# Delta rule of a block kernel: where the inverse of 32 x 32 diagonal blocks is formed, and one level of block products taken out

## The chip, the cores and the metric

The program runs on one core of a Trainium2 chip. The metric is the device time of one execution in microseconds (us); for the kernel before it is the median of three runs.

## The reference, cut to what matters

The program is one pass of a three-layer block network over 512 tokens of width 1024. Its first layer mixes a windowed attention with a gated delta rule of eight heads; later stages are a mixture of experts, two more mixers and feed-forward layers. The change is in the delta rule alone. In the reference it works in chunks of 64 tokens: from keys, a gate and a decay it forms a strictly lower triangular matrix A per chunk and head, and needs the inverse of the unit triangular matrix I + A:

```python
a_mat = jnp.where(tril_strict, jnp.einsum('nbhid,nbhjd->nbhij', kbeta, kc) * decay_mat, 0.0)
eye = jnp.eye(CHUNK, dtype=jnp.float32)
t_mat = lax.linalg.triangular_solve(eye + a_mat, jnp.broadcast_to(eye, a_mat.shape),
                                    left_side=True, lower=True, unit_diagonal=True)
u = jnp.einsum('nbhij,nbhjd->nbhid', t_mat, vc * bc[..., None])
w = jnp.einsum('nbhij,nbhjd->nbhid', t_mat, kbeta * jnp.exp(gcum)[..., None])
```

`u` and `w` then enter a recurrence over the chunks that carries a 128 x 128 state.

## The kernel before, in words

The kernel takes chunks of 128 tokens, so four chunks make the 512 tokens, and every per-chunk matrix of a head lies in one tile of 128 partitions x 512 columns, chunk c in columns 128c to 128c + 127. `dn_head(h)` computes one head. It is a generator: each `yield` hands back a weight, and `first_mixer` weaves the eight heads with the attention's generator by these weights. The first part of a head, up to `yield None`, projects q, k and v (three weight slabs of 128 x 1024, each 24 matmuls on 512 columns, L295), normalizes them, and forms `at`, the transposed triangular matrix of all four chunks (L551). The second part inverts, runs the recurrence and writes `ob[h]`. The second part of head h - 1 is woven into the first part of head h, and behind the three projections of head h in the program's text.

The inverse is built from small blocks to large ones. GpSimd inverts the 16 x 16 diagonal blocks: SP stores `at` to DRAM (`blk[0]`, L560) and loads the 32 diagonal blocks back with four DMAs, one block per partition (`sub`, L565). Fifteen steps of a multiply and a subtract on 32 partitions (L571, L573; at most 64 elements each) leave the inverses. Four DMAs store them to the diagonal blocks of a second DRAM tensor that is zero elsewhere (L575), and one DMA loads all of it as tile `t` (L577). TensorE transposes `t` into `tt` (L496, `tokmajor`), and two levels follow, i = 4 (blocks of 16 to 32) and i = 5 (32 to 64). A level is: GpSimd masks `at` to the off-diagonal blocks of that size (`xm`, L555), four chunk products of `xm` and `t` on TensorE (`pcps`, L547), a copy on ScalarE (`ty`), four products of `ty` and `tt`, a subtraction from `tt` on VectorE, a transposition of `tt` on TensorE and a copy to `t` on ScalarE. A float32 product of 128 columns shows as two instructions, so a set of four products shows as eight. A last level, 64 to 128, works on the one block that is left (L603, L609).

The products of the weights use a split of every float32 into two parts: a slab is loaded by SP into one of two `wraw` buffers (L278), cast by ScalarE (`whi`, L282), the rest formed by VectorE (`wlo`, L286); `whi` and `wlo` have two buffers each. SP's queue is worked off in order: a DMA that waits holds all behind it.

The order of each engine's instructions is fixed when the program is built. A planner goes through all instructions with the order in the text as their rank, and gives an engine the first in rank of those that it takes to be ready by then. So an instruction that stands late in the text can be put early, when what it needs is there and its engine is free; the order doesn't change while the program runs.

Of the kernel before, what the change touches and what calls it, by code (L numbers as in the profile page):

```python
# [22 lines left out]
F32 = mybir.dt.float32  # L23
# [4 lines left out]
OP = mybir.AluOpType  # L28
# [3 lines left out]
P = 128  # L32
S = 512
# [44 lines left out]
def _consts():  # L78
    p = np.arange(P)
    f = np.float32  # L80
    eye = (p[:, None] == p[None, :]).astype(f)
    neg = lambda ok: np.where(ok, f(0), f(NEG)).astype(f)
    c = {}
    c["ident"] = eye
    c["m_up"] = neg(p[:, None] <= p[None, :])
    c["m_lo"] = neg(p[:, None] >= p[None, :])
    c["m_prev"] = neg(p[None, :] >= p[:, None])
    c["m_res"] = neg((p[:, None] // 32 == p[None, :] // 32) & (p[:, None] >= p[None, :]))
    c["tri"] = (p[:, None] <= p[None, :]).astype(f)
    c["half"] = (p[:, None] // 64 == np.arange(2)[None, :]).astype(f)  # L90
    for i in range(7):
        b = 1 << i
        ok = (p[:, None] // (2 * b) == p[None, :] // (2 * b)) & (p[:, None] // b % 2 == 0) & (p[None, :] // b % 2 == 1)
        c[f"lv{i}"] = ok.astype(f)
    x = np.arange(3 + 512)
    c["un1"] = (x[None, :] - 3 == 4 * p[:, None]).astype(f)
    x = np.arange(12 + 512)
    c["un2"] = (x[None, :] - 12 == 16 * (p[:, None] % 32) + p[:, None] // 32).astype(f)
    return c


_CONSTS = _consts()
_COFF = {}
_n = 0
# [114 lines left out]
class Kern:  # L219
# [230 lines left out]
        self.hb = t("hb")  # L450
        nc.vector.tensor_scalar(self.hb, self.beta, 0.5, None, op0=OP.mult)

    @staticmethod
    def diag(t, c):

        a = t[:, c * P : (c + 1) * P]
        return bass.AP(a.tensor, a.offset, [[16 * S + 16, 8], [S, 16], [1, 16]])

    def dn_head(self, h):

        nc, dl, pa = self.nc, self.dl, self.pa

        def T(tag, dt=F32):
            return dl.tile([P, S], dt, tag=tag, name=tag, bufs=2 if tag in DN2 else 1)
# [11 lines left out]
        for j in range(3):  # L476
# [4 lines left out]
            w = lambda i: self.V("conv_w", i * 24 + j * 8 + h)  # L481
# [5 lines left out]
            o = T("s" + "qkv"[j])  # L487
# [22 lines left out]
        r = dl.tile([P, 8], F32, tag="rqk", name="rqk", bufs=2)  # L510
# [39 lines left out]
        at, aq = T("at"), T("aq")  # L550
# [5 lines left out]
            return x  # L556


        blk, eng = self.blk[h % 2], self.sub_engine
        nc.sync.dma_start(blk[0], at)  # L560
        x = self.sm.tile([P, S], F32, tag="sq", name="sub", bufs=2)
        lm = dl.tile([32, 64], F32, tag="lm", name="lm")
        La, Lt = (x[0:32, i * 256 : (i + 1) * 256].rearrange("p (i k) -> p i k", k=16) for i in range(2))
        for c in range(4):
            nc.sync.dma_start(La[8 * c : 8 * c + 8], self.diag(blk[0], c))  # L565
        eng.memset(Lt, 0.0)
        eng.memset(x[0:32, 256:512:17], 1.0)
        for j in range(15):
            n, w = 15 - j, j + 1
            m = lm[0:32, 0 : n * w].rearrange("p (i k) -> p i k", k=w)  # L570
            eng.tensor_tensor(m, La[:, j, j + 1 :][:, :, None].to_broadcast([32, n, w]),  # L571
                              Lt[:, j, 0:w][:, None, :].to_broadcast([32, n, w]), op=OP.mult)
            eng.tensor_sub(Lt[:, j + 1 :, 0:w], Lt[:, j + 1 :, 0:w], m)  # L573
        for c in range(4):
            nc.sync.dma_start(self.diag(blk[1], c), Lt[8 * c : 8 * c + 8])  # L575
        tt, t_ = T("tt"), T("t")
        nc.sync.dma_start(t_, blk[1])  # L577
        nc.vector.tensor_mul(aq, per_chunk(sk, sq_), dec)
        yield 0.9
        rowmul(qd, sq_, [self.egc[:, c, h : h + 1] for c in range(4)])  # L580
# [2 lines left out]
        nc.vector.tensor_tensor(c4(bv), c4(pv), colb(self.hb), op=OP.mult)  # L583
        yield 0.5
        yield None
        with self.tc.issue_after(self.last_mm.ins):
            ps = tokmajor(t_)
        nc.scalar.copy(tt, ps)
        yield 0.2
        for i in (4, 5):  # L590
            x = masked(i)
            y = T("ty")
            nc.scalar.copy(y, per_chunk(x, t_))
            yield 0.9
            nc.vector.tensor_sub(tt, tt, per_chunk(y, tt))
            yield 0.9
            nc.scalar.copy(t_, tokmajor(tt))
            yield 0.2

        a, b = slice(0, 64), slice(64, 128)  # L600
# [16 lines left out]
        for c in range(4):  # L617
            t = slice(c * P, (c + 1) * P)
# [19 lines left out]
        for c in range(4):  # L638
            t = slice(c * P, (c + 1) * P)
# [14 lines left out]
        r = self.rsqrt(dl, v, 4, "or")  # L654
# [9 lines left out]
        z, th = T("cy"), T("cth")  # L664
# [238 lines left out]
    def first_mixer(self):  # L903
        nc, tc = self.nc, self.tc
        with ExitStack() as c0:
# [4 lines left out]
            with ExitStack() as c1:  # L910
                self.pa = c1.enter_context(self.pool("pmix", 3, PSUM))
                self.ptag = "da"

                hi, lo = self.wslab(None, D, raw=self.raw0)
                ps = self.pm.tile([P, S], F32, tag="mm", name="mm")
                for k in range(KD):
                    self.split(self.x[k], self.xh[k], self.xl[k], self.V("norm_mix", k))
                    w = slice(k * P, (k + 1) * P)
                    self.gemm(ps, hi[:, w], lo[:, w], self.xh[k : k + 1], self.xl[k : k + 1], 1, first=k == 0, last=k == KD - 1)
                for k in range(KD):  # L920
                    self.square_step(k)
                self.lead = []
                self.lead = [ps, self.xgemm("w_dn", 1)]
                self.norm_end()
                self.dk = dk = c1.enter_context(self.pool("dk", 1))
                self.dl = c1.enter_context(self.pool("dl", 1))
                self.at = at = c1.enter_context(self.pool("at", 1))
                self.mb = {}

                def load(n):  # L930
                    o, w = _COFF[n]
                    t = dk.tile([P, w], F32, tag="craw", name="craw", bufs=1)
                    nc.scalar.dma_start(t, self.I["consts"][:, o : o + w])
                    return t

                for n in ("m_up", "m_res", "m_lo", "m_prev", "lv4", "lv5"):
                    self.mb[n] = dk.tile([P, P], BF, name="b" + n)
                    nc.gpsimd.tensor_copy(self.mb[n], load(n))
                for n in ("tri",):
                    w = _COFF[n][1]  # L940
                    self.mb[n] = dk.tile([P, w], F32, name="b" + n)
                    nc.scalar.dma_start(self.mb[n], self.I["consts"][:, _COFF[n][0] : _COFF[n][0] + w])
                self.on = [at.tile([P, S], F32, name=f"on{g}") for g in range(3)]
                self.stat = [at.tile([P, 4, 2, 2], F32, name=f"stat{g}") for g in range(3)]
                dram = c1.enter_context(self.pool("blk", 1, bass.MemoryType.DRAM))
                self.blk = [[dram.tile([P, S], F32, name=f"blk{i}{j}") for j in range(2)] for i in range(2)]
                z = self.sm.tile([P, S], F32, tag="sq", name="zsq")
                nc.gpsimd.memset(z, 0.0)
                for i in range(2):
                    nc.scalar.dma_start(self.blk[i][1], z)  # L950
                self.sub_engine = nc.gpsimd
                self.cin = self.dl.tile([P, S + 4], F32, name="cin")
                nc.gpsimd.memset(self.cin[:, 0:4], 0.0)
                self.gqk = at.tile([P, 1], F32, name="gqk")
                nc.vector.tensor_mul(self.gqk, self.V("q_norm"), self.V("k_norm"))
                self.mask0 = at.tile([P, 4 * P], BF, name="mask0")
                for i, n in enumerate(("m_prev", "m_lo", "m_prev", "m_lo")):
                    nc.gpsimd.tensor_copy(self.mask0[:, i * P : (i + 1) * P], self.mb[n])
                def heads():

                    gen = [self.dn_head(h) for h in range(8)]

                    def first(h):
                        c = next(gen[h])
                        while c is not None:
                            yield c
                            c = next(gen[h])

                    for h in range(8):
                        for _ in range(3):  # L970
                            yield next(gen[h])
                        if h == 0:
                            self.dn_scalars()
                            yield from first(h)
                        else:
                            yield from self.interleave((first(h), 1.0), (gen[h - 1], 1.0))
                    yield from gen[7]

                self.weave((heads(), DN_T), (self.attention(), AT_T))
# [1166 lines left out]
```

## Time and profile before

| what | value |
|---|---|
| median of three runs | 2274.68 us (2271.39 to 2280.24) |
| the profiled execution, its time | 2271.66 us |
| its span, first to last instruction | 2269.9 us |
| TensorE busy | 2164.8 us, 95% of the span |
| VectorE, ScalarE, GpSimd busy | 1488.8, 966.8, 438.9 us |
| mean granted clock of TensorE | 0.982 |
| substitution of the eight heads on GpSimd | first instruction at 82.2 us, last at 645.6 us |

The 1.8 us between the span and the profiled execution's time lie around the instructions. PE is TensorE's matmuls, DVE VectorE, ACT ScalarE, POOL GpSimd, and SPq the DMA queue of SyncE. Matmuls are pipelined: one on 512 columns is shown as 0.39 us long, while the next starts 0.23 us after it. So a set's price is read from start to start rather than from the durations.

### The profile page before, as it was taken

The numbers are of one execution on the slowest core, as the hardware profiler recorded it, in microseconds if no ns is written. First come the engines' busy times: TensorE is split into PE (matmuls) and PEld (weight loads), VectorE is DVE, ScalarE is ACT, GpSimd is POOL, SyncE is SP. The second block draws the span as 40 slices with busy tenths as digits, with TensorE's granted clock in tenths as the row PEclk, the third lists the DMA queues.
The fourth block names the chain that finished last, engine by engine and source line by source line (L and its number), as shares of the span: only waits on it lengthen the run. The fifth ranks groups of instructions, "written<-read, shape, count | busy, mean of one in ns | idle before, by whom it ended". The sixth has DMA issues, their size and how long they took to land.

```text
span 2269.9 us, 28779 instructions
## 1 busy us (share of the span) xinstructions
PE 2164.8 (95%) x10718; PEld 1722.2 (76%) x10718; DVE 1488.8 (66%) x2674; ACT 966.8 (43%) x1594; POOL 438.9 (19%) x616
## 2 busy tenths in 40 slices
PE   8999999999999998999897899999999889999997
PEld 6777777878777886565686677788888778888886
DVE  6766666666755446775689877847477567777533
ACT  4434434444343234565455454424334235444321
POOL 1222012022021013101327049700230220000000
PEclk9999999999999999899998999999999999999998
DMA  4221121211212246799321012233223113232332
GB/s 156 67 61 54 66 67 49 74 58 48 75 43 79 93 143 244 271 360 313 117 91 59 29 41 90 93 96 99 85 96 94 55 34 107 94 101 93 98 94 87
DMA packets 83299, 231.14 MB, mean 102 GB/s; under 512 B 18576, under 2 KB 22288, under 8 KB 83152
## 3 DMA queue, kind: packets, MB, share of 16 engines
q1 hardware_dynamic: 78048, 217.02, 28.8%
q0 software_dynamic: 2944, 10.49, 1.5%
q10 hardware_dynamic: 2160, 1.71, 0.3%
q8 instruction: 87, 1.43, 0.3%
q14 instruction: 60, 0.49, 0.1%
HBM read 215.89 MB, written 12.65 MB: 101 GB/s over the span
## 4 chain that ended last, share of the span: by engine, by line
PE 38%; DVE 10%; ACT 2%; issue 1%; POOL 0%; DVEq 0%; ACTq 0%; POOLq 0%
PE mm L295 34%; DVE wlo L286 2%; DVE cvps L1702 2%; DVE fy L1778 1%; PE po L1653 1%; DVE xl L306 1%; PE psc L1622 0%; PE st L1480 0%; ACT whi L282 0%; PE gps L1926 0%; PE ppt L1646 0%; DVE fe L1773 0%; DVE t L2035 0%; PE mm L1996 0%; PE mm L1997 0%
## 5 line engine op out<-in xcount | busy, mean ns | idle before, releaser
L295 PE MATMUL mm<-xh,whi 128*128 128x512 f32 x1664 | 662.5, 399 | 13.3 <-ACT whi L282 12.8
L295 PE MATMUL mm<-xh,wlo 128*128 128x512 f32 x1664 | 661.1, 398 | 9.1 <-DVE wlo L286 9.0
L295 PE MATMUL mm<-xl,whi 128*128 128x512 f32 x1664 | 659.0, 396 | 6.3 <-DVE xl L303 3.9
L282 ACT CAST whi<-wraw 128x1024 fp32r<-128x1024 f32 (+4 forms) x311 | 300.6, 967 | 512.8 <-PE mm L295 409.3
L286 DVE TENSOR_TENSOR wlo<-wraw,whi 128x1024 fp32r<-128x1024 f32 (+4 forms) x311 | 367.1, 1181 | 130.9 <-ACT whi L282 122.3
L295 PEld LDWEIGHTS mm<-xh,wlo 128*128 128x128 f32 x1664 | 314.7, 189 | 79.6 <-DVE wlo L286 14.5
L295 PEld LDWEIGHTS mm<-xh,whi 128*128 128x128 f32 x1664 | 314.9, 189 | 78.4 <-ACT whi L282 14.6
L295 PEld LDWEIGHTS mm<-xl,whi 128*128 128x128 f32 x1664 | 315.4, 190 | 73.6 <-DVE xl L306 5.9
L1778 DVE SCALAR_TENSOR_TENSOR fy<-fe,par,fy 128x512 f32<-128x512 f32 x176 | 141.9, 807 | 3.7 <-ACT fy L1776 0.6
L295 PE MATMUL mm<-ah,whi 128*128 128x512 f32 x352 | 137.8, 392 | 0.2 <-ACT ah L302 0.2
L295 PE MATMUL mm<-al,whi 128*128 128x512 f32 x352 | 137.5, 391 | 0.0
L295 PE MATMUL mm<-ah,wlo 128*128 128x512 f32 x352 | 137.3, 390 | 0.0
L1773 DVE TENSOR_TENSOR fe<-mm,rb 128x512 f32<-128x512 f32 x88 | 60.3, 687 | 72.3 <-PE mm L295 69.4
L295 PEld LDWEIGHTS mm<-ah,whi 128*128 128x128 f32 x352 | 66.0, 188 | 15.9 <-ACT ah L302 1.4
L295 PEld LDWEIGHTS mm<-al,whi 128*128 128x128 f32 x352 | 66.1, 188 | 14.3 <-DVE al L303 0.4
L295 PEld LDWEIGHTS mm<-ah,wlo 128*128 128x128 f32 x352 | 66.1, 188 | 13.9
L1776 ACT ACTIVATE fy<-fe,par 128x512 f32<-128x512 f32 x88 | 71.7, 814 | 9.2 <-DVE fe L1773 8.6
L302 ACT CAST ah<-fy 128x512 fp32r<-128x512 f32 x44 | 27.3, 621 | 112.6 <-DVE fy L1782 112.6
L1794 DVE TENSOR_TENSOR x<-x,mm 128x512 f32<-128x512 f32 x32 | 22.0, 688 | 79.6 <-PE mm L295 79.6
L555 POOL TENSOR_TENSOR xm<-at,blv 128x512 f32<-128x512 f32 x16 | 19.6, 1226 | 258.8 <-PE pcps L547 207.7
L1115 DVE TENSOR_TENSOR xl<-wraw,xh 128x1024 fp32r<-128x1024 f32 x40 | 48.9, 1223 | 26.6 <-ACT xh L1114 25.8
L777 ACT ACTIVATE pe<-psc,nm,rq 128x128 f32<-128x128 f32 (+1 forms) x96 | 45.4, 481 | 48.4 <-DVE nm L772 37.9
(746 smaller groups left out, 3676.0 us busy)
## 6 DMA issues: line engine op xcount, KB each, us to landing
wraw<-in_w_up SPq DMA_DIRECT2D x88, 512.0 KB
wraw<-in_w_eu SPq DMA_DIRECT2D x64, 512.0 KB
wraw<-in_w_dn SPq DMA_DIRECT2D x48, 512.0 KB
wraw<-in_w_qkv SPq DMA_DIRECT2D x36, 512.0 KB
wraw<-in_w_ed SPq DMA_DIRECT2D x32, 512.0 KB
wraw<-in_w_g SPq DMA_DIRECT2D x16, 512.0 KB
wraw<-in_w_l SPq DMA_DIRECT2D x16, 512.0 KB
wraw<-in_w_dn SPq DMA_DIRECT2D x16, 448.0 KB
```

The lines of the kernel that those rows point to most:

```text
L282: nc.scalar.copy(hi, raw)
L286: nc.vector.tensor_sub(lo, raw, hi.bitcast(F32))
L295: self.last_mm = nc.tensor.matmul(ps, w, x, start=first and n == 0, stop=last and n == tot - 1)
L302: nc.scalar.copy(hi, src)
L306: nc.vector.scalar_tensor_tensor(lo, src, scale, hi.bitcast(F32), op0=OP.mult, op1=OP.subtract)
L777: nc.scalar.activation(pe[:, o : o + n], psc[:, o : o + n], AF.Exp, bias=nm[:, i : i + 1], scale=rq[:, b, e : e + 1], accum_out=stat[:, b, ...
L1115: (nc.gpsimd if self.ncv < 5 else nc.vector).tensor_sub(lo, raw, hi.bitcast(F32))
L1653: nc.tensor.matmul(po[:, e, :], pts[e][:, c * P : (c + 1) * P], v1[:, c, h * 64 : h * 64 + 64], start=c == 0, stop=c == b)
L1702: nc.vector.scalar_tensor_tensor(yp, u[:, j : j + S], w(j), yp, op0=OP.mult, op1=OP.add)
L1773: nc.vector.tensor_mul(e[:, 2:], ps, self.rb)
L1776: nc.scalar.activation(y, e[:, 2:], AF.Identity, scale=w(2), bias=self.V(f"l{i}_fcb", f))
L1778: nc.vector.scalar_tensor_tensor(y, e[:, t : t + S], w(t), y, op0=OP.mult, op1=OP.add)
```

## The change

GpSimd now inverts the 32 x 32 diagonal blocks, of which the 512 tokens have sixteen, and level i = 4 is left out of the loop. Eight partitions work on one block, each on four of its columns (`rows4` holds the unit columns that the substitution begins with). Eight DMAs store the parts of `at` with 64 bytes a run so that two loads bring each block, repeated, to its eight partitions: `la` for columns 16 to 31, then for 0 to 15. Thirty-one steps of a multiply and a subtract on 128 partitions follow, with 4i elements in step i (31 down to 1). The store of the result, a memset of `t` and four loads of `t` stand in the second part of the head, ahead of a `yield 2.0`; `issue_after` ties to TensorE's last matmul only what a block issues on TensorE itself, and the new block issues nothing there. Two preset zero tensors in DRAM, the mask `lv4` and the tile `lm` go.

```diff
+    c["rows4"] = (x[None, :] % 32 == 4 * (p[:, None] % 8) + x[None, :] // 32).astype(f)
...
-        blk, eng = self.blk[h % 2], self.sub_engine
-        nc.sync.dma_start(blk[0], at)
-        x = self.sm.tile([P, S], F32, tag="sq", name="sub", bufs=2)
-        lm = dl.tile([32, 64], F32, tag="lm", name="lm")
-        La, Lt = (x[0:32, i * 256 : (i + 1) * 256].rearrange("p (i k) -> p i k", k=16) for i in range(2))
-        for c in range(4):
-            nc.sync.dma_start(La[8 * c : 8 * c + 8], self.diag(blk[0], c))
-        eng.memset(Lt, 0.0)
-        eng.memset(x[0:32, 256:512:17], 1.0)
-        for j in range(15):
-            n, w = 15 - j, j + 1
-            m = lm[0:32, 0 : n * w].rearrange("p (i k) -> p i k", k=w)
-            eng.tensor_tensor(m, La[:, j, j + 1 :][:, :, None].to_broadcast([32, n, w]),
-                              Lt[:, j, 0:w][:, None, :].to_broadcast([32, n, w]), op=OP.mult)
-            eng.tensor_sub(Lt[:, j + 1 :, 0:w], Lt[:, j + 1 :, 0:w], m)
-        for c in range(4):
-            nc.sync.dma_start(self.diag(blk[1], c), Lt[8 * c : 8 * c + 8])
-        tt, t_ = T("tt"), T("t")
-        nc.sync.dma_start(t_, blk[1])
+        ab, tb = self.blk[h % 2]
+        eng = self.sub_engine
+        for b in range(4):
+            for i, n in ((1, 32), (0, 16)):
+                o = 32 * b + 16 * i
+                nc.sync.dma_start(bass.AP(ab.tensor, ab.offset + 8192 * i + 64 * n * b, [[16, n], [16 * n, 4], [1, 16]]),
+                                  c4(at)[32 * b : 32 * b + n, :, o : o + 16])
+        La = [None, None]
+        for i, n in ((1, 32), (0, 16)):
+            la = self.sm.tile([P, S], F32, tag="sq", name="la", bufs=2)
+            nc.sync.dma_start(la[:, 0 : 16 * n], bass.AP(ab.tensor, ab.offset + 8192 * i, [[16 * n, 16], [0, 8], [1, 16 * n]]))
+            La[i] = la.rearrange("p (k i) -> p k i", i=16)
+        x = dl.tile([P, 2, P], F32, tag="sub", name="sub")
+        nc.sync.dma_start(x[:, 0, :], self.I["consts"][:, _COFF["rows4"][0] : _COFF["rows4"][0] + P])
+        Lt = x[:, 0, :].rearrange("p (r k) -> p r k", r=4)
+        for i in range(31, 0, -1):
+            m = x[:, 1, 0 : 4 * i].rearrange("p (r k) -> p r k", r=4)
+            eng.tensor_tensor(m, La[i // 16][:, 0:i, i % 16][:, None, :].to_broadcast([P, 4, i]),
+                              Lt[:, :, i][:, :, None].to_broadcast([P, 4, i]), op=OP.mult)
+            eng.tensor_sub(Lt[:, :, 0:i], Lt[:, :, 0:i], m)
...
         yield None
+        tt, t_ = T("tt"), T("t")
+        with self.tc.issue_after(self.last_mm.ins):
+            nc.sync.dma_start(tb, x[:, 0, :])
+            eng.memset(t_, 0.0)
+            for b in range(4):
+                nc.sync.dma_start(c4(t_)[32 * b : 32 * b + 32, :, 32 * b : 32 * b + 32],
+                                  bass.AP(tb.tensor, tb.offset + 4096 * b, [[32, 32], [1024, 4], [1, 32]]))
+        yield 2.0
         with self.tc.issue_after(self.last_mm.ins):
             ps = tokmajor(t_)
         nc.scalar.copy(tt, ps)
         yield 0.2
-        for i in (4, 5):
+        for i in (5,):
...
-                for n in ("m_up", "m_res", "m_lo", "m_prev", "lv4", "lv5"):
+                for n in ("m_up", "m_res", "m_lo", "m_prev", "lv5"):
...
-                self.blk = [[dram.tile([P, S], F32, name=f"blk{i}{j}") for j in range(2)] for i in range(2)]
-                z = self.sm.tile([P, S], F32, tag="sq", name="zsq")
-                nc.gpsimd.memset(z, 0.0)
-                for i in range(2):
-                    nc.scalar.dma_start(self.blk[i][1], z)
+                self.blk = [[dram.tile([P, P], F32, name=f"blk{i}{n}") for n in (0, 1)] for i in range(2)]
```

## Rows read from the trace of the kernel before

**Rows 1.** The page, busy time: us, share of the span, instructions.
```profile
PE 2164.8 (95%) x10718; PEld 1722.2 (76%) x10718; DVE 1488.8 (66%) x2674; ACT 966.8 (43%) x1594; POOL 438.9 (19%) x616
```

**Rows 2.** Windows: engines' busy time, granted clock, DMA share, GB/s.
```profile
60.00:640.00 580.00, 568.62 (x3275) 455.46 (x3274) 379.61 (x901) 243.61 (x517) 111.15 (x274) 1.00 0.19 62
640.00:700.00 60.00, 57.13 (x350) 44.97 (x349) 33.25 (x88) 28.89 (x64) 12.19 (x21) 1.00 0.14 45
700.00:780.00 80.00, 80.00 (x350) 65.21 (x349) 38.94 (x43) 23.05 (x30) 5.15 (x4) 1.00 0.29 96
```

**Rows 3.** Timeline of PE in head 1's first level: start, us, instruction.
```profile
190.85 1.13 PE L547 MATMUL pcps<-t,xm 128*128 128x128 f32 x8
191.81 0.60 PE L687 MATMUL hrow<-ident,hx 128*128 128x128 f32 x4
...
197.86 1.05 PE L547 MATMUL pcps<-tt,ty 128*128 128x128 f32 x8
198.75 1.06 PE L547 MATMUL pcps<-kb,sk 128*128 128x128 f32 x8
...
200.79 0.60 PE L496 MATMUL tmps<-ident,tt 128*128 128x128 f32 x4
201.22 0.49 PE L724 MATMUL qst<-ident,q 128*128 128x128 f32 x3
```

**Rows 4.** POOL's groups by form: busy us, mean ns, idle before.
```profile
L540 POOL TENSOR_TENSOR dec<-dec,rqk 128x512 f32<-128x512 f32 x8 | 8.4, 1053 | 70.2 <-ACT dec L539 70.2
...
L573 POOL TENSOR_TENSOR sub<-sub,lm 32x15 f32<-32x15 f32 x16 | 3.5, 220 | 1.3
L571 POOL TENSOR_TENSOR lm<-sub 32x15 f32<-32x15 f32 x16 | 3.3, 206 | 49.3 <-DMA sub<-blk 48.6
L573 POOL TENSOR_TENSOR sub<-sub,lm 32x64 f32<-32x64 f32 x8 | 2.5, 316 | 0.6
L571 POOL TENSOR_TENSOR lm<-sub 32x64 f32<-32x64 f32 x8 | 2.3, 292 | 0.6
```

**Rows 5.** Timeline of POOL, head 2: substitution's first and last, then L668.
```profile
207.76 0.21 POOL L571 TENSOR_TENSOR lm<-sub 32x15 f32<-32x15 f32 x1 [6.18 <-DMA sub<-blk]
...
218.56 0.21 POOL L573 TENSOR_TENSOR sub<-sub,lm 32x15 f32<-32x15 f32 x1
...
233.55 1.27 POOL L668 TENSOR_TENSOR ob<-ob,cy 128x512 f32<-128x512 f32 x1 [6.61 <-DVE ob L659]
```

**Rows 6.** Timeline of SP's queue, heads 0, 2 and 7.
```profile
97.52 0.34 SPq L577 DMA_DIRECT2D t<-blk  x1
...
201.92 0.33 SPq L560 DMA_DIRECT2D blk<-at  x1
...
212.41 0.36 SPq L278 DMA_DIRECT2D wraw<-in_w_dn  x1
...
221.56 0.34 SPq L577 DMA_DIRECT2D t<-blk  x1
230.59 0.36 SPq L278 DMA_DIRECT2D wraw<-in_w_qkv  x1
...
648.49 0.34 SPq L577 DMA_DIRECT2D t<-blk  x1
```

**Rows 7.** SP's waits, 60 to 720 us: total, times, longest.
```profile
SPq L575 <- POOL sub L573: 64.4, 8, 13.8
```

**Rows 8.** Timeline of PE: transpositions of t, heads 0, 2, 7; head 7's second level.
```profile
109.28 0.60 PE L496 MATMUL tmps<-ident,t 128*128 128x128 f32 x4
...
273.83 0.60 PE L496 MATMUL tmps<-ident,t 128*128 128x128 f32 x4
...
657.51 0.49 PE L496 MATMUL tmps<-ident,t 128*128 128x128 f32 x3
...
667.86 1.06 PE L547 MATMUL pcps<-t,xm 128*128 128x128 f32 x8
```

**Rows 9.** Timeline of ACT: the cast of the slab loaded at 230.59.
```profile
246.60 1.05 ACT L282 CAST whi<-wraw 128x1024 fp32r<-128x1024 f32 x1 [2.68 <-PE mm L295]
```

More of the change, by code (lines that the diff above doesn't have):

```diff
@@ L98, in _consts @@
     c["un2"] = (x[None, :] - 12 == 16 * (p[:, None] % 32) + p[:, None] // 32).astype(f)
+    x = np.arange(P)
+    c["rows4"] = (x[None, :] % 32 == 4 * (p[:, None] % 8) + x[None, :] // 32).astype(f)
     return c
@@ L451, in dn_scalars @@
         nc.vector.tensor_scalar(self.hb, self.beta, 0.5, None, op0=OP.mult)
[L453 to L457, printed above, removed]
     def dn_head(self, h):
```

## The prediction

> **What bounds the kernel now.** I read the busy times first. TensorE is busy for 95% of the span, GpSimd for 19% [rows 1]: only what takes time from TensorE, or makes it wait, can move the end. Next come the windows over the delta rule. [...] So the stage that holds the change is bound by TensorE's own queue, with 14.3 us idle in 640, and what the stage gains passes on: the work behind 700 us hangs on the same engine and starts when the stage ends. A busy TensorE isn't one at its peak, since a lone matmul shows its whole pipeline as busy. The third view is therefore TensorE's timeline, read from start to start [rows 3]. Then come GpSimd's groups and timeline for the price of a step [rows 4, 5], SP's timeline and waits for what stands in its queue [rows 6, 7], and the places where `t` is used, for the time to spare [rows 8].
>
> **Removed: one level on TensorE.** In head 1 the first set of products takes 191.81 - 190.85 = 0.96 us until the next instruction starts, the second 198.75 - 197.86 = 0.89 us, the transposition 201.22 - 200.79 = 0.43 us [rows 3]. That is 2.28 us a head, and 8 x 2.28 = 18.2 us over eight. The lower bound takes both sets at the smaller price, 8 x 2.21 = 17.7 us; the upper takes the whole durations shown, 1.13 + 1.05 + 0.60 = 2.78 us, or 22.2 us. Nothing is a lower bound only if TensorE waited elsewhere for as long; that is the rivals' business. I take 18.2, the start-to-start price, since other work is queued right behind each of the three. The level's mask on GpSimd, two copies on ScalarE and the subtraction on VectorE go too. These engines are busy for 111, 244 and 380 of 580 us [rows 2], so I count nothing for them. The setup's memset, mask and two stores of zeros lie before this stage: nothing.
>
> **Moved and grown: the substitution.** On 32 partitions a multiply of 15 elements takes 206 ns and one of 64 takes 292; a subtract 220 and 316 [rows 4]. So a multiply costs 180 ns plus 1.755 ns an element, a subtract 191 ns plus 1.96. At 512 elements the first line gives 1079 ns, and the multiply L540 of that length on 128 partitions takes 1053 [rows 4]: partitions cost nothing, elements do. The new steps have 4 x (1 + ... + 31) = 1984 elements for each kind. Multiplies: 31 x 0.180 + 1984 x 0.001755 = 9.06 us; subtracts: 31 x 0.191 + 1984 x 0.00196 = 9.81 us. For gaps: head 2's thirty instructions run from 207.76 to 218.77, 11.0 us [rows 5], where the same formula (680 elements of each kind) gives 8.1; the rest is 0.097 us an instruction, so 6.0 for 62. Together 24.9 us against 11.0, or +13.9 us a head. What the formula leaves open is the multiply's operand `la`, read at a step of 64 bytes; the multiplies in the rows read theirs packed or repeated. Between nothing and twice the part that grows with elements lie 0 and +3.5 us; I take 0, because no row shows the step to matter, and keep +3.5 for the late ends below.
>
> [...]
>
> **The DMAs around it.** SP's store of `at` starts 5.8 us ahead of the first step on GpSimd (201.92 to 207.76) [rows 5, 6]. Eight stores at 0.33 us each in place of one put 2.3 us more in front, three loads in place of four take 0.3 away: +2.0 us. Behind the substitution one store replaces four and four loads one: nothing. Thus `t` is complete 13.9 + 2.0 = 16 us later than now. The short runs of 64 and 128 bytes cost no more than that as long as the DMA engines idle: their share is 0.19 [rows 2].
>
> **Where that lies.** In head 2 the load of `t` goes out at 221.56 and its transposition comes at 273.83 [rows 6, 8], 52 us later, since three projections of the next head and the attention stand between. With 16 us more, and 3 for landing (half of the 5.8 us above, which holds two trips), 33 us are left; heads 1 to 6 stand alike. The two ends have no such cover. In head 0 the load goes out at 97.52 and the transposition starts at 109.28: 97.5 + 16 + 3 = 116.5, so 7 us too late. In head 7 it is 648.49 and 657.51: 667.5, 10 us too late [rows 6, 8]. Against that, the missing level shortens the chain behind `t`: in head 7 from 657.51 to the next level's products at 667.86 [rows 8], 10.3 us. The ends of both chains thus hardly move; what can be lost is the wait itself, if nothing else stands in TensorE's queue there. Bounds: 0 if the planner moves the transposition back behind other work, 17 us if it leaves it in place. The nearest row says that the planner knows GpSimd's pace: in head 2 it placed a weight load at 212.41 ahead of the store that waits for the substitution [rows 6], so it expected the substitution to end later than that, with the true end at 218.8. I take 3 us.
>
> **SP's queue.** SP already waits for the substitution 64.4 us in eight times, at most 13.8 [rows 7], without a gap in TensorE. A store placed as now holds SP 16 us longer. Behind it stands the next weight load, in head 2 at 230.59, 9 us after the load of `t`, and that slab is cast at 246.60 [rows 6, 9]: 9 + 16.0 - 3 for landing is 22 us of cover, 6 more than needed. Counted at nothing. `ob`'s product (L668), next on GpSimd, starts at 233.55, and the new substitution ends at 207.76 + 2 + 24.9 = 234.7 [rows 5]: 1 us late, nobody waits at once.
>
> **Sum.** -18.2 + 3 = -15 us. The profiled execution would go from 2271.7 to 2256.5 us. It lies 3 us under the median of the runs, so for the median 2274.7 - 15 = 2259 us, 0.7% less. A measurement of this kernel tells about 0.5%, 11 us, from no change.
>
> **The rivals.**
> *The ends eat the gain.* The transpositions of heads 0 and 7 stay where they are and TensorE waits for them, 7 + 10 us, or 24 with the slow operand. For it: order is fixed ahead of the run, and these two heads have 9 to 12 us now. Against it: row 212.41, and there is other work for TensorE at both places. Time: 2275 - 18 + 10 to 18, 2267 to 2275 us.
> *SP starves the weights: slower.* The store stands ahead of a weight load that is needed sooner than head 2's. From 700 to 780 us, where slabs follow each other, TensorE starts 350 matmuls in 80 us, 0.23 us each [rows 2], so a slab of 24 is 5.5 us, and a load two slabs ahead has 11 - 3 = 8 us of cover: of 16 us of delay 8 reach TensorE. It decides from the point where the losses pass 18 us, three heads; in five heads it costs 40 us: 2275 - 18 + 40 = 2297 us. For it: the waits of rows 7 are there now. Against it: the store now ranks behind the next head's projections, and in head 2 the cover holds.
> *The level cost more than its instructions.* Every set that is put between slabs also breaks their rhythm; at whole durations and no wait the gain is 22, with some of the stage's 14 us idle 24 to 28: 2247 to 2252 us.
>
> **How the numbers follow.** The likeliest, 2252 to 2266, holds 0.57; the eaten gain 0.24; the starved queue 0.13; more than counted 0.06. To leave out no more than two in ten, the range runs from 2248 to 2281: it takes in the first two whole and the near edge of the slower one. Faster by over 0.5% is below 2263: most of the likeliest and all of the last, 0.57. Within 0.5%: the eaten gain and the likeliest's edge, 0.30. Slower: 0.13.
>
> **What would show it.** L547 `pcps<-t,xm` and `pcps<-tt,ty` at 64 instructions each; some 62 instructions of substitution in 24 to 28 us a head; TensorE's busy time 18 to 22 us lower and its idle time from 60 to 700 us no more than 5 above 14.3. I am wrong if TensorE's waits name the transposition of `t` with several us in heads 0 and 7, or `mm` waits for casts while SP waits for the substitution 25 us at a time, or a multiply of 124 elements takes far over 0.4 us.

## The result: 1.2% slower, and the profile after

The changed kernel takes 2301.94 us in the median (2300.58 to 2303.96) beside 2274.09 for the kernel before in the same comparison: a ratio of 1.0122, with a 95% interval from 1.0108 to 1.0135. That is 28 us more where I forecast 15 less, and it lies above the range, which ended at 2281. The profiled execution took 2300.58 us; its span grew from 2269.9 to 2298.8 us, by 28.9.

The page's first part, busy times of the changed kernel:

```profile
PE 2158.5 (94%) x10558; PEld 1712.3 (74%) x10558; DVE 1484.0 (65%) x2666; ACT 957.2 (42%) x1578; POOL 545.8 (24%) x854
```

Beside [rows 1], TensorE has 160 instructions fewer, just the 8 x 20 of the level. Its busy time fell by 6.3 us only, and its idle time in the span rose from 105.1 to 140.3 us, by 35.2. The two sum to the 28.9 us of the span. So the question is where 35 us of waiting come from, and why busy time fell by 6 and not by 18.

Windows of the changed kernel: the three stages of [rows 2], then five windows of 10 us (columns as there):

```profile
60.00:640.00 580.00, 543.14 (x3019) 432.19 (x3018) 365.73 (x858) 229.25 (x489) 200.32 (x466) 0.97 0.18 60
640.00:700.00 60.00, 48.15 (x300) 37.91 (x298) 26.72 (x74) 20.16 (x46) 26.91 (x66) 0.91 0.15 48
700.00:780.00 80.00, 78.40 (x378) 63.31 (x378) 42.59 (x81) 28.98 (x48) 7.72 (x6) 1.00 0.23 78
120.00:130.00 10.00, 3.55 (x15) 3.21 (x16) 1.92 (x2) 3.43 (x8) 1.04 (x1) 0.51 0.51 160
170.00:180.00 10.00, 3.73 (x19) 2.89 (x17) 2.42 (x8) 1.58 (x3) 1.27 (x2) 0.91 0.41 125
340.00:350.00 10.00, 5.12 (x18) 3.84 (x17) 3.96 (x5) 2.78 (x4) 0.00 (x0) 0.66 0.47 166
520.00:530.00 10.00, 5.31 (x23) 3.82 (x24) 2.95 (x5) 3.24 (x4) 0.00 (x0) 0.66 0.47 166
680.00:690.00 10.00, 3.23 (x13) 2.64 (x14) 0.00 (x0) 1.17 (x2) 3.75 (x9) 0.50 0.17 39
```

TensorE idles 36.9 us from 60 to 640 and 11.8 from 640 to 700, 48.7 together where it was 14.3; from 700 to 780 it is 1.6 where it was nothing. The five windows of 10 us show that the loss isn't spread out: TensorE is busy there for 3.2 to 5.3 of 10 us. They also show a second loss. The granted clock, 1.00 in all three stages of [rows 2], has a mean of 0.50 to 0.91 in them; the trace's record of it holds two levels, 1.00 and 0.50. The level's 18.2 us should have come off the busy time and 6.3 did, so some 12 us of busy time came back, in instructions that run slower (three of the transposition take 0.88 us at 686.77, and 0.49 in [rows 8]). The record of the clock gives nearly as much: where it is at 0.50 between 60 and 700 us, TensorE is busy for 21.3 us in sum, which at half speed is an estimated loss of 10.6 us.

TensorE's timeline of the changed kernel, the instructions behind its long gaps (in brackets: us of idle time, and what ended it):

```profile
122.53 1.09 PE L492 MATMUL tmps<-ident,t 128*128 128x128 f32 x4 [4.22 <-DMA t<-blk]
127.53 2.05 PE L543 MATMUL pcps<-t,xm 128*128 128x128 f32 x8 [3.92 <-issue]
...
180.14 1.12 PE L693 MATMUL hrow<-ident,hx 128*128 128x128 f32 x4 [6.41 <-ACT hx L690]
...
344.88 0.59 PE L760 MATMUL psc<-bm_res,idb 128*128 128x512 bf16 x1 [7.93 <-ACT vt L723]
...
524.69 1.97 PE L800 MATMUL po<-pt,vt 128*64 128x128 f32 x8 [6.04 <-ACT pt L791]
...
686.77 0.88 PE L492 MATMUL tmps<-ident,t 128*128 128x128 f32 x3 [10.93 <-DMA t<-blk]
```

There are two kinds. At 122.53 and 686.77 it is `t` itself that TensorE waits for, in heads 0 and 7, the two ends. At 180.14, 344.88 and 524.69, in heads 1, 3 and 5, what TensorE waits for has nothing to do with the delta rule's inverse: ScalarE's `hx`, `vt`, `pt`. (The gap at 127.53, in head 0, comes last.) What made ScalarE late is seen in head 3. SP's timeline of the changed kernel:

```profile
316.47 0.36 SPq L280 DMA_DIRECT2D wraw<-in_w_dn  x1
336.07 0.34 SPq L586 DMA_DIRECT2D blk<-sub  x1
337.68 1.75 SPq L589 DMA_DIRECT2D t<-blk  x4
339.47 0.43 SPq L569 DMA_DIRECT2D sub<-in_consts  x1
340.01 0.37 SPq L280 DMA_DIRECT2D wraw<-in_w_qkv  x1
```

VectorE's timeline, the last reader of that weight buffer:

```profile
324.98 1.23 DVE L288 TENSOR_TENSOR wlo<-wraw,whi 128x1024 fp32r<-128x1024 f32 x1
```

ScalarE's timeline, from the cast of that slab on:

```profile
343.30 1.04 ACT L284 CAST whi<-wraw 128x1024 fp32r<-128x1024 f32 x1 [11.25 <-DMA wraw<-in_w_qkv]
344.25 0.58 ACT L723 COPY vt<-vtps 128x512 f32<-128x512 f32 x1
```

The buffer of `wraw` is free at 326.2 us. The weight load that takes it goes out at 340.0, since the store of the substitution's result stands ahead of it in SP's queue and goes out when GpSimd is done, at 336.07, with four loads of `t` and one of the unit columns right behind. ScalarE waits 11.25 us for the slab, and `vt`, for which TensorE waits, stands behind the cast in ScalarE's queue. So "TensorE waits for `vt`" reads: it waits for GpSimd, through SP and ScalarE. Heads 1 and 5 go alike: ScalarE's cast there waits 8.99 and 6.59 us for a slab whose load went out behind the store, and `pt` stands right behind the cast, `hx` 2.0 us behind it.

The gap at 127.53 looks like a wait for `t`, but `t` was there at 122.53, and the profile names no engine that ended it. Read from the kernel, these chunk products need one of three buffers in PSUM (tag `da`, L463), by their order the one that ScalarE's `dec` reads; and `dec`, which ends at 127.43, stands behind a cast. ScalarE's timeline:

```profile
125.35 1.04 ACT L284 CAST whi<-wraw 128x1024 fp32r<-128x1024 f32 x1 [9.52 <-DMA wraw<-in_w_qkv]
126.30 1.13 ACT L535 ACTIVATE dec<-dps,ngc 128x128 f32<-128x128 f32 x4
```

SP's timeline, the load of that slab behind the store:

```profile
117.91 0.33 SPq L586 DMA_DIRECT2D blk<-sub  x1
...
121.77 0.37 SPq L280 DMA_DIRECT2D wraw<-in_w_qkv  x1
```

The slab's buffer was free at 101.1 us, when VectorE's `wlo` had read it. So SP's queue starves the weights in head 0 as well, and both kinds meet there.

SP's waits from 60 to 720 us (total, times, longest) say how much of that there is:

```profile
SPq L586 <- POOL sub L575: 161.4, 8, 27.5
```

Beside [rows 7], SP stands 161 us for the substitution, up to 27.5 at a time, where it was 64 and 13.8.

The page's groups of the substitution, multiply and subtract, all forms, eight heads:

```profile
L573 POOL TENSOR_TENSOR sub<-la,sub 128x124 f32<-128x124 f32 (+30 forms) x248 | 95.2, 384 | 34.6 <-DMA la<-blk 15.9
L575 POOL TENSOR_TENSOR sub<-sub 128x124 f32<-128x124 f32 (+30 forms) x248 | 93.0, 375 | 19.4
```

Two of GpSimd's groups by form, the longest step's:

```profile
L573 POOL TENSOR_TENSOR sub<-la,sub 128x124 f32<-128x124 f32 x8 | 3.7, 461 | 15.9 <-DMA la<-blk 15.9
...
L575 POOL TENSOR_TENSOR sub<-sub 128x124 f32<-128x124 f32 x8 | 3.4, 429 | 0.6
```

That is 11.9 us of multiplies and 11.6 of subtracts a head. From its first instruction to its last a substitution takes 26.8 us (head 6) to 31.7 (head 0), 28.5 in the mean of eight.

### The profile page after: what moved, and what is told of

Read it like the earlier page. It is cut to its first block, busy times and chain, and to the rows that moved or that the text cites. A ratio compares the mean times of both kernels' runs of the same rounds, so it can differ in the third digit from the quotient of the medians.

```text
span 2298.8 us, 28734 instructions
## 1 busy us (share of the span) xinstructions
PE 2158.5 (94%) x10558; PEld 1712.3 (74%) x10558; DVE 1484.0 (65%) x2666; ACT 957.2 (42%) x1578; POOL 545.8 (24%) x854
## 3 DMA queue, kind: packets, MB, share of 16 engines
q1 hardware_dynamic: 83424, 217.42, 27.9%
## 4 chain that ended last, share of the span: by engine, by line
PE 39%; DVE 8%; ACT 2%; issue 1%; POOL 0%; DVEq 0%; POOLq 0%; ACTq 0%
PE mm L297 35%; DVE cvps L1704 1%; DVE wlo L288 1%; DVE fy L1780 1%; PE po L1655 1%; PE psc L1624 0%; PE st L1482 0%; PE gps L1928 0%; PE ppt L1648 0%; ACT whi L284 0%; DVE t L2037 0%; PE mm L1998 0%; PE mm L1999 0%; PE mm L2000 0%; DVE xl L308 0%
## 5 line engine op out<-in xcount | busy, mean ns | idle before, releaser
L297 PE MATMUL mm<-xh,whi 128*128 128x512 f32 x1664 | 663.5, 400 | 13.4 <-ACT whi L284 12.9
L573 POOL TENSOR_TENSOR sub<-la,sub 128x124 f32<-128x124 f32 (+30 forms) x248 | 95.2, 384 | 34.6 <-DMA la<-blk 15.9
L575 POOL TENSOR_TENSOR sub<-sub 128x124 f32<-128x124 f32 (+30 forms) x248 | 93.0, 375 | 19.4
L297 PEld LDWEIGHTS mm<-ah,wlo 128*128 128x128 f32 x352 | 66.1, 188 | 14.3
L304 ACT CAST ah<-fy 128x512 fp32r<-128x512 f32 x44 | 27.3, 621 | 112.6 <-DVE fy L1784 112.6
```

The lines of the kernel that those rows point to most:

```text
L297: self.last_mm = nc.tensor.matmul(ps, w, x, start=first and n == 0, stop=last and n == tot - 1)
L304: nc.scalar.copy(hi, src)
L573: eng.tensor_tensor(m, La[i // 16][:, 0:i, i % 16][:, None, :].to_broadcast([P, 4, i]), Lt[:, :, i][:, :, None].to_broadcast([P, 4, i]), o ...
L575: eng.tensor_sub(Lt[:, :, 0:i], Lt[:, :, 0:i], m)
```

## The experiments

The theory: the substitution's length is the cause, and it costs twice, by SP's queue (heads 1, 3, 5, and a part in head 0) and by the late `t` (heads 0, 7), while the level itself was priced rightly. The rivals: the change's DMAs or its partitions cost the time, or the missing level isn't worth what its instructions take. Gains and losses in us are differences of medians to the kernel before in the same comparison; the change itself stands at +27.9.

**The level alone.** The kernel before, its one level left out:

```diff
-        for i in (4, 5):
+        for i in (5,):
```

> The kernel before with level i = 4 left out of the loop and nothing put in its place, so that the inverse lacks the products from 16 to 32. It measures what the level is worth alone. By the sum of the prediction: 18 us less, 2254 to 2259 us. If the level was hidden in TensorE's idle time: under 8 us less, 2266 to 2275 us.

Measured: 2259.53 us, ratio 0.9934 (0.9916 to 0.9952), -13.5 us. TensorE's timeline of this run has one new gap of some size:

```profile
670.81 1.11 PE L687 MATMUL hrow<-ident,hx 128*128 128x128 f32 x4 [2.97 <-ACT hx L684]
```

The window from 640 to 700 us has a granted clock of 0.91 here. Idle time from 60 to 700 us is 15.3 us, 1.0 above that of before. The span is 12.2 shorter: TensorE's busy time fell by 15.6 us and its idle time rose by 3.4, most of that outside the stage. The 2.6 us that the busy time lacks to 18.2 I put to the lower clock of that window, where TensorE is busy for 6.9 us at a clock of 0.50; no experiment shows it. The level is worth about its start-to-start price.

**The substitution alone.** The kernel before, with 36 more GpSimd instructions behind its own steps:

```diff
+        for _ in range(36):
+            eng.tensor_scalar(Lt, Lt, 1.0, None, op0=OP.mult)
         for c in range(4):
             nc.sync.dma_start(self.diag(blk[1], c), Lt[8 * c : 8 * c + 8])
```

> The kernel before with its substitution made some 20 us a head longer by 36 multiplications of the result by one on GpSimd; level, DMAs and all else as before. Theory A: SP's wait for the substitution grows from 64 to some 200 us and weight loads come late: 2295 to 2325 us. If only the way in which the change uses t (late loads in the second part, the memset ahead of the substitution) is at fault, the longer substitution alone costs at most the ends: 2275 to 2290 us, with no gaps of TensorE in the middle heads.

Measured: 2427.39 us, ratio 1.068 (1.0657 to 1.0704), +154 us, much more than expected. GpSimd's groups show why:

```profile
L575 POOL TENSOR_SCALAR sub<-sub 32x256 f32<-32x256 f32 x288 | 257.8, 895 | 23.4
```

One such instruction takes 895 ns, so the substitution became 47 us long in the mean, not some 31, and the size says nothing on the change. What it does say is the kind: SP's waits and two places of TensorE's timeline,

```profile
SPq L577 <- POOL sub L575: 233.6, 7, 46.1
```

```profile
136.46 1.12 PE L496 MATMUL tmps<-ident,t 128*128 128x128 f32 x4 [23.29 <-DMA t<-blk]
...
398.29 0.58 PE L756 MATMUL psc<-bm_res,idb 128*128 128x512 bf16 x1 [18.71 <-ACT vt L719]
```

With level, stores and loads as before and only the substitution longer, the same two kinds of gap stand at the same places: `t` in head 0, and the product that stood at 344.88 in the changed kernel, which waits for `vt` again.

**All but the length.** The change with the first 15 of the 31 steps left out, so with every DMA, the late store and the missing level:

```diff
-        for i in range(31, 0, -1):
+        for i in range(16, 0, -1):
```

> The changed kernel with sixteen of the thirty-one steps of the substitution (the first fifteen are left out, so the blocks aren't inverted), which by the measured steps take some 11 us, as long as the substitution before; all DMAs, the late store, the memset and the missing level stay. Theory A (the length of the substitution is the cause): no gap of TensorE over 2 us, 2254 to 2266 us. If the more numerous DMAs, the memset or the place of the store are at fault by themselves: over 2275 us.

Measured: 2257.49 us, ratio 0.9925 (0.991 to 0.994), -17.3 us. The substitution takes 10.7 us (head 2) to 16.1 (head 0), 12.2 in the mean, and TensorE's idle time from 60 to 700 us is 18.1, 3.8 above before. SP still waits for GpSimd, and longer than in [rows 7]:

```profile
SPq L586 <- POOL sub L575: 103.4, 8, 15.9
```

Against the expectation one gap of TensorE over 2 us is left, in head 0, where the substitution is longest:

```profile
114.27 1.12 PE L492 MATMUL tmps<-ident,cth 128*128 128x128 f32 x4 [5.87 <-ACT cth L502]
```

It is the queue's kind again: the store goes out at 102.66, a weight load behind it at 106.54, and ScalarE's cast waits 6.57 us for that slab. Elsewhere SP's wait costs nothing that shows while it is short, and neither do the eight stores with short runs or the 128 partitions. This falsifies the rivals: with a short substitution the change is a gain of about the level's 18.2 us.

**The store on GpSimd's queue.** If SP's queue is what starves the weights, taking the store and the loads of `t` from it should give that part back:

```diff
-            nc.sync.dma_start(tb, x[:, 0, :])
+            nc.gpsimd.dma_start(tb, x[:, 0, :])
...
-                nc.sync.dma_start(c4(t_)[32 * b : 32 * b + 32, :, 32 * b : 32 * b + 32],
+                nc.gpsimd.dma_start(c4(t_)[32 * b : 32 * b + 32, :, 32 * b : 32 * b + 32],
```

> The changed kernel, but GpSimd issues the store of the result and the four loads of t itself, right behind its substitution, so that nothing in SP's queue waits for the substitution. Theory A (SP, held 15 to 28 us a head behind the store, hands out the weight loads late, and TensorE runs out of slabs in heads 1, 3 and 5): TensorE's idle at those three places goes (6.4 + 7.9 + 6.0 us and some 10 us of lowered clock), the time falls from 2302 to 2275 to 2285 us, and the waits for t in heads 0 and 7 stay (4 and 11 us). Theory B (the late t at the two ends is the whole loss): 2298 to 2303 us.

Measured: 2302.65 us, ratio 1.012 (1.0102 to 1.0138), +29.7 us: no gain. SP's waits show that the edit missed its aim:

```profile
SPq L569 <- DMA blk<-sub: 157.4, 7, 30.3
```

The load of the next head's unit columns goes into the same, single buffer `sub`, so it waits until the store has read it. The wait moved from line 586 to line 569 and stayed on SP. Next I gave `sub` a second buffer and the products a tile of their own:

```diff
-        x = dl.tile([P, 2, P], F32, tag="sub", name="sub")
+        x = dl.tile([P, P], F32, tag="sub", name="sub", bufs=2)
+        mt = dl.tile([P, P], F32, tag="lm", name="lm")
```

> The first experiment (store and loads of t issued by GpSimd) with two buffers for the tile sub, so that SP's load of the unit columns for the next head waits for the store of the head before last. In the first experiment that load had taken over the whole wait (157 us of SP's time against 161). Theory A (whatever holds SP until the substitution ends makes the weights late): now nothing on SP waits for the substitution, TensorE's gaps in heads 1, 3 and 5 go, 2272 to 2284 us. Theory B (the substitution disturbs the weights in another way, by GpSimd's or the DMA engines' own work): the gaps stay, 2298 to 2305 us.

Measured: 2304.5 us, ratio 1.0128 (1.0105 to 1.0151), +29.7 us. A miss again, by the same line of the waits:

```profile
SPq L570 <- DMA blk<-sub: 139.2, 6, 30.0
```

With two buffers that load is placed further ahead, and still waits for a store. The third edit moves the load of the unit columns to GpSimd's queue too, so that nothing on SP depends on the substitution:

```diff
-        nc.sync.dma_start(x, self.I["consts"][:, _COFF["rows4"][0] : _COFF["rows4"][0] + P])
+        nc.gpsimd.dma_start(x, self.I["consts"][:, _COFF["rows4"][0] : _COFF["rows4"][0] + P])
```

> The sixth experiment with the load of the unit columns on GpSimd too, so that no DMA left on SP waits for the substitution, at any place of its queue; heads 0 and 7 as in the change. Theory A: the gaps in heads 1, 3 and 5 go (6.2 + 7.5 + 5.3 us and some 10 us of clock): 2272 to 2284 us, with t still awaited at the ends (8 and 13 us). Theory B (the weights are late for another reason than SP's queue): 2297 to 2306 us.

Measured: 2283.22 us, ratio 1.0039 (1.0027 to 1.0052), +10.1 us, or 19.6 less than the run before it. SP's waits name the substitution no more, the largest gap in heads 1 to 6 is 1.82 us, and TensorE's timeline keeps these:

```profile
126.20 1.09 PE L492 MATMUL tmps<-ident,t 128*128 128x128 f32 x4 [7.46 <-DMA t<-blk]
...
671.61 0.87 PE L492 MATMUL tmps<-ident,t 128*128 128x128 f32 x3 [13.41 <-DMA t<-blk]
```

The gaps of heads 1, 3 and 5 went with SP's wait, and so did head 0's second one: its weight load goes out at 101.45 here. The waits for `t` at the ends stayed and grew.

**The store behind the weight loads.** The same aim, on SP's own queue: the change orders the store behind a matmul, which holds nothing on SP; here it is ordered behind the last weight load that stands ahead of it in the text.

```diff
-            nc.sync.dma_start(raw, src)
+            self.last_raw = nc.sync.dma_start(raw, src)
...
-        with self.tc.issue_after(self.last_mm.ins):
+        with self.tc.issue_after(self.last_raw.ins):
             nc.sync.dma_start(tb, x[:, 0, :])
```

> The changed kernel with one tie more: on SP the store of the result and the loads of t stay behind the last weight load that stands ahead of them in the text (in the change the tie is to a matmul, which ties nothing on SP). Theory A: no weight load waits for the substitution, TensorE's three gaps in heads 1, 3 and 5 go, the time falls to 2260 to 2280 us; in heads 0 and 7 t comes no earlier. Theory B: no change in the middle heads, 2298 to 2305 us.

Measured: 2277.72 us, ratio 1.0019 (1.0008 to 1.003), +4.7 us: 23 us came back. SP's timeline in head 3:

```profile
318.74 0.36 SPq L280 DMA_DIRECT2D wraw<-in_w_qkv  x1
325.86 0.33 SPq L280 DMA_DIRECT2D wraw<-in_w_dn  x1
331.11 0.33 SPq L280 DMA_DIRECT2D wraw<-in_w_qkv  x1
331.49 0.42 SPq L586 DMA_DIRECT2D blk<-sub  x1
```

In head 3 the weight loads now go out as their buffers come free, ahead of the store. Not so in head 0: the load that the change held until 121.77 stands behind the store in the text too, goes out at 121.88, and both gaps of that head are still there (4.26 and 3.80 us). What is left of the loss is at the ends, as head 7 in TensorE's timeline:

```profile
663.49 0.87 PE L492 MATMUL tmps<-ident,t 128*128 128x128 f32 x3 [11.24 <-DMA t<-blk]
```

**The transposition later.** If the late `t` costs because its transposition is placed too early, more work ahead of it in heads 0 and 7 should help:

```diff
-        yield 2.0
+        yield {0: 12.0, 7: 12.0}.get(h, 2.0)
```

> The second experiment with more work in the text ahead of the transposition of t in heads 0 and 7 (a yield of 12 in place of 2). The wait in head 0 goes if attention and the next head's projections fill it: 8 us and some 5 of clock less. In head 7 little is left to fill with. 2262 to 2272 us; if there is nothing to fill with at either end, 2275 to 2280 us.

Measured: 2287.7 us, ratio 1.006 (1.0046 to 1.0073), +12.9 us, 8 worse than without the edit. Head 7 by the timelines of GpSimd, ScalarE and TensorE:

```profile
675.12 1.26 POOL L848 TENSOR_TENSOR oa<-oa,on 128x512 f32<-128x512 f32 x1
```

```profile
676.42 0.62 ACT L304 CAST oah<-oa 128x512 fp32r<-128x512 f32 x1 [12.30 <-POOL oa L848]
```

```profile
681.43 1.12 PE L269 MATMUL orps<-ident,ory 128*128 128x128 f32 x4 [12.02 <-DVE ory L661]
```

The work that was to fill the gap passes through GpSimd itself: the attention's sum `oa` comes in GpSimd's queue between the last steps of the substitution and right behind them, and is done at 676.4. ScalarE's cast of `oa` waits for it, VectorE's work waits 11.21 us for the cast, and TensorE waits for VectorE until 681.43. In head 0 a weight load still stands behind the store: SP waits 22.3 us for the substitution, until 118.63, the load goes out at 122.49, and TensorE idles 9.7 us until 131.02. Moving the consumer doesn't cover the long substitution here.

**The ends by the old way.** The run with the store behind the loads, heads 0 and 7 with the 16 x 16 substitution, their own store pair and both levels:

```diff
+        ends = h in (0, 7)
+        if ends:
+            blk, eng = self.blo, self.sub_engine
...
-        for i in (5,):
+        for i in (4, 5) if ends else (5,):
```

> The second experiment (store behind the weight loads, 2278 us) with heads 0 and 7 done as in the kernel before: 16 x 16 blocks and both levels. Theory: what the second experiment still loses lies at these two ends (t awaited for 4.3 + 3.8 and 11.2 us, and about 10 us of lowered clock); six heads keep the level's 2.28 us each. 2273 - 13.7 = 2256 to 2266 us, less than both kernels. If the ends aren't what is left: 2270 to 2280 us.

Measured: 2261.78 us, ratio 0.9938 (0.9924 to 0.9951), -13.0 us: faster than both kernels. Its windows:

```profile
60.00:640.00 580.00, 568.62 (x3227) 453.98 (x3230) 386.09 (x908) 242.14 (x513) 201.37 (x469) 1.00 0.20 64
640.00:700.00 60.00, 57.16 (x331) 45.35 (x330) 35.38 (x87) 27.45 (x59) 7.58 (x6) 1.00 0.16 53
```

TensorE's idle time and, to two digits, the clock are those of [rows 2] again, with GpSimd busy for 201 us where it was 111: GpSimd's longer work by itself costs nothing that shows. Six heads without the level would give 6 x 2.28 = 13.7 us; 13.0 were measured, with an interval from 11.1 to 17.3.

**Each loss by itself.** Two runs complete the square. With only head 7 by the old way (`ends = h == 7`):

> The best kernel so far (store behind the weight loads, heads 0 and 7 as before, 2262 us), but only head 7 as before. Head 0's late t (4 + 4 us of gap, some 5 us of clock) comes back, its level's 2.3 us are saved: 2266 to 2274 us. If the two ends together cost by head 7 alone: 2258 to 2263 us.

Measured: 2270.96 us, ratio 0.9989 (0.9978 to 1.0), -2.2 us. So head 7's new form costs 4.7 + 2.2 = 6.9 us net and head 0's 13.0 - 2.2 = 10.8. TensorE's timeline keeps head 0's two gaps, the first of them here, and head 7 has none:

```profile
123.94 1.09 PE L498 MATMUL tmps<-ident,t 128*128 128x128 f32 x4 [5.08 <-DMA t<-blk]
```

And with both ends by the old way but the store where the change has it (`issue_after(self.last_mm.ins)`):

> The change with heads 0 and 7 as before and nothing else: in heads 1 to 6 the store and the loads of t keep their place on SP. If the loss of the change is the sum of two, the ends (2278 - 2262 = 16 us) and SP's queue (2302 - 2278 = 24 us), this comes to 2302 - 16 = 2286 us, 2281 to 2290, with the gaps in heads 1, 3 and 5 still there. If the queue does no harm without the late ends: 2260 to 2270 us.

Measured: 2283.54 us, ratio 1.0042 (1.0025 to 1.0059), +10.4 us. TensorE's timeline has the gaps of heads 1, 3 and 5, as this one:

```profile
337.28 0.59 PE L789 MATMUL psc<-bm_res,idb 128*128 128x512 bf16 x1 [8.07 <-ACT vt L752]
```

The two losses add up, to 0.2 us; each cell is known to some 2.5 to 4 us, so this is closer than the measurement carries:

| us against the kernel before | ends new | ends as before |
|---|---|---|
| store as in the change | +27.9 | +10.4 |
| store behind the loads | +4.7 | -13.0 |

SP's queue costs 23.2 us with the new ends and 23.4 with the old, in heads 1 to 6, since in head 0 the moved store changes nothing; the ends cost 17.5 us with the store as in the change and 17.7 with it behind the loads. The ends' cost is a net one: by the old way these two heads keep their level, 2 x 2.28 = 4.6 us of work, so their waits cost 22.2, by the same reckoning 9.2 in head 7 and 13.1 in head 0. By the trace of the changed kernel the three gaps there sum to 19.1 us, and 7.4 us of busy time at the lower clock add an estimated 3.7. Not all of that is the late `t`: head 0's second gap, 3.9 us, is the queue's. In the run with nothing on SP that gap went, but `t` came later there, so no run prices the two in that head apart. The sum is then -18.2 + 23.3 + 22.2 = +27.3 us, where +27.9 were measured.

## Why the prediction was wrong, point by point

**TensorE bounds the stage, and what it gains passes on.** Right [rows 2]: -13.5, -17.3 and -13.0 us in three runs that leave levels out came through to the end.

**The level, 18.2 us in eight heads.** Right. With a short substitution 17.3 us are gained, and 13.0 in six heads where 13.7 were due.

**The substitution, 24.9 us.** Mis-sized: 28.5 in the mean. At the longest form a multiply takes 461 ns, against 180 + 1.755 x 124 = 398 by my line, a subtract 429 against 191 + 1.96 x 124 = 434. So the line holds for the subtract, which doesn't read `la`, and I put the multiply's 63 ns, or 0.5 ns an element, to the read of `la` at a step of 64 bytes, which I had counted at nothing. 1984 elements make 1.0 us a head, an estimate: no run varies that step alone. The rest is in both kinds alike: the subtracts sum to 11.6 us a head against 9.8, because single instructions of the same form are longer now and then. The subtract of 56 elements takes 0.29 to 0.32 us in six heads, 1.32 in head 2 and 1.24 in head 5. I didn't test why.

**`t` 16 us later.** Too little. In head 0 the first step starts 9.2 us behind the first store of `at` (76.95 to 86.14), where it was 4.8 before (77.32 to 82.16): +4.4 and not the +2.0 of the sum, since the eight stores hold SP 4.39 us, 0.55 each where I took 0.33. The substitution takes 31.7 us there. The first load of `t` goes out at 119.45 in place of 97.52, 22 us later, and the transposition starts at 122.53 in place of 109.28; I had 116.5.

**"Where that lies", the ends: "I take 3 us".** This step failed. The two ends cost 22.2 us where I took 3. The waits for `t` themselves, 4.2 and 10.9 us, are near my 7 and 10, and under the bound of 17; the rest is the lowered clock and, in head 0, a held weight load (3.9 us). I let the waits go for a planner that I read, from one row [rows 6], as knowing GpSimd's pace. In that row the order was right by 6 us at a substitution of 11; it is no evidence for one of 28. And the filler isn't free: when I moved the transposition myself, what stood in its place needed GpSimd.

**"SP's queue. Counted at nothing."** This step failed as well, and costs as much: 23 us in heads 1 to 6, and a part of head 0's. The mechanism was the one of the rival "SP starves the weights", down to the waits of rows 7; its price was too high (40), its chance too low (0.13). Where I went wrong is the cover. I worked it out for head 2, 22 us where 16 were needed [rows 6, 9], and passed it to the others. In heads 1, 3 and 5 the weight load is due sooner: in head 3 its buffer is free at 326.2 and the load held until 340.0, 13.8 us, 8 of which reach TensorE. The order on SP is visible; that the planner put the store there because it expected the substitution to end sooner is inferred, since its own times show in no trace.

**Rivals.** "The ends eat the gain" happened as well. (Its time was reckoned with a loss of 10 to 18 us beside a stated price of 17 to 24; the price gives 2274 to 2281 us.) "The level cost more than its instructions" didn't show: 13.5 and 17.3 us came back without it. I had the rivals as alternatives; two of them came together, and the loss of both, 45.5 us, is two and a half times the gain.

**What was in no step.** The lowered clock in and behind the gaps: some 11 to 12 of the 45.5 us, by TensorE's busy time. I counted a gap at its length, and it costs more.

## What to carry to other kernels

An issuing queue that serves both prefetched loads and the result of a slow step hands the growth of that step to the loads as soon as their cover is used up (here SP's wait grew from 64.4 to 161.4 us, and 23 us reached the end), so put the dependent transfer behind the loads that come free earlier, with an order on the queue that issues it (23.2 us came back here), and look at every transfer that the slow step releases, the refill of its buffer too. Work out the cover for the tightest place, not for one; where a chain has no cover, as at the first and the last head, keep the short form there. An engine at 19% isn't free if something else waits for it in order: its long step also delays the short work behind it (in the run with the later transposition ScalarE's cast waited 12.30 us for GpSimd's `oa`).

## What the runs showed of the hardware that was not expected

In and behind gaps of 4 to 11 us the granted clock was below 1.00: 0.91, 0.66 and 0.66 in the windows of heads 1, 3 and 5, and 0.51 and 0.50 in those of the two ends, nearly throughout the lower of the two recorded levels. The transposition behind the gap at 686.77 took 0.88 us for three instructions where [rows 8] have 0.49 at head 7. In the change the lower clock took back some 11 to 12 of the 18 us of busy time that the missing level saves.

A subtract of 124 elements took 429 ns on 128 partitions, where the line through the forms on 32 partitions [rows 4] gives 434: in these forms elements count on GpSimd, partitions don't. The kind of instruction counts too: the 36 added multiplications by a constant, of 256 elements on 32 partitions, took 895 ns each, where the line for a multiply of two tensors gives 629.
